# Thirty-two experts in 12 units instead of 13: four more of them in blocks of 64 rows

## The chip, the cores and the metric

The kernel runs on one core of one Trainium2 chip. Its time is device microseconds of one execution, from launch to end; lower is better. Five engines take part: TensorE (PE, with its weight loads as PEld), VectorE (DVE), ScalarE (ACT), GpSimd (POOL), and SyncE (SP), which issues the DMAs. Each works through its own list of instructions in order.

## The reference, cut to what matters

Two transformer blocks over 512 tokens of 1024 columns, in fp32. The change lies in the first block's mixture of experts:

```python
logits = xf @ w_router + b_router                 # 512 tokens, 32 experts
top_val, top_idx = lax.top_k(logits, 4)           # four experts a token: 2048 pairs
gates = softmax(top_val)
# for each expert, over its tokens:
hu = xb @ w_up[e] + b_up[e]                       # 1024 -> 2048 columns
act = x_glu * sigmoid(1.702 * x_glu) * (x_lin + 1)   # x_glu, x_lin: clipped halves of hu
y = act @ w_down[e] + b_down[e]                   # 1024 -> 1024
# a token's four rows, times their gates, are added up
```

How many tokens an expert gets depends on the data. With the inputs that the reference draws, its router gives the experts, after the first two (numbers 0 and 1, with 53 and 122 tokens), in falling order: 192, 133, 105, 104, 95, 87, 84, 79, 77, 73, 70, 67 (these are the ranks 2 to 13), 64, 63, 60, 53 (ranks 14 to 17), then 53, 50, 49, 48 down to 10 (ranks 18 to 31).

## The kernel before, in words

Matmuls are made of fp32r products: each operand is split in a high part and a low part, and a product is hi·hi + hi·lo + lo·hi (`mm3`, L290 to L292). The weights of an expert, 12 MB, come in 12 tiles of 128x2048 by DMA into a ring of six. ACT copies each tile into its high part `wh` (L281), and DVE subtracts that to give the low part `wl` (L286). Of an expert's 12 tiles, two are subtracted on POOL instead (L284).

Experts are worked in the order of a list, `units`. A unit is 256 rows of gathered tokens (`xT`, one buffer), cut in blocks. A block has 128 or 64 rows, all of one expert. There are three kinds of unit: a **pair** is two experts with 128 rows each; a **mixed** unit is one with 128 rows and two with 64; a **dual** unit is one expert with 128 + 64 rows and one with 64. `cap` says how many tokens of each rank have a place in these blocks. Tokens beyond it go to further blocks of 128 rows, which a loop on the chip works through after the second unit, as often as a number counted from the data says (`NXi`); each pass loads that expert's weights again through two half tiles.

For each unit, DVE makes one-hot columns (`hot`, L1083), PE gathers the tokens with them (L1125), and ACT and DVE copy the halves into `xT` (L1130). The small instructions L1100 to L1111 make each block's row numbers and gates. All of this for the next unit is issued during the current one. Then per expert: `expert_up` in four chunks of 256 hidden columns, `split_T`, and `expert_down` while the next expert's `expert_up` runs.

A block of 128 rows and one of 64 differ in these lines:

- PE: with 128 rows each step is the three matmuls L290 to L292. With 64 rows the hi and lo columns of the rows lie side by side, so that one matmul makes hi·hi and lo·hi in the two halves of the partitions, and a second one hi·lo: two matmuls (L1173, L1174, or L1168 and L1171 in the first step).
- DVE, per chunk, with 128 rows: L1208, L1210 and L1212 read the sum where it lies, in PSUM (`bank_hu`), and L1211 reads SBUF. With 64 rows the two halves are added first: ACT copies one into SBUF (`ft`, L1204), DVE adds the other (L1205), and L1208, L1210 and L1212 read `ft`.
- Behind: `split_T` has one DVE instruction L1230 for 64 rows and two for 128. A block of 64 is gated with two ACT and two DVE instructions (L1248, L1249), one of 128 with two ACT instructions (L1259).

The order of the instructions on each engine is fixed when the program is built, by a scheduler with its own estimate of durations; across the engines they wait for each other by semaphores.

Of the kernel before, what the change touches and what calls it, by code (L numbers as in the profile page):

```python
# [16 lines left out]
T = 512  # L17
# [5 lines left out]
SMALL = 18  # the experts by rank: from 2 up to 192 tokens for two of them, 64 from this one on, else 128  # L23
# [204 lines left out]
def tile_block(ctx, tc, A, out, dbg=None):  # L228
# [23 lines left out]
    # eight banks of PSUM, in groups that are used in turn  # L252
# [83 lines left out]
    def gemv(src, cofs, gp, bufs):  # L336
        """silu(c) @ src; columns 256 q .. 256 q + 255 end up in row 32 q"""
# [9 lines left out]
    def gemv_split(src, cofs, gp, ring_raw, nv=4):  # L347
        """the same, with the products and most of the sums on the other engines"""
# [35 lines left out]
    def mod_row(i, src, cofs, gp, bias, plus=0.0, mul=None, how="split"):  # L384
        """row i of md_d: (silu(c) @ src + bias + plus) * mul"""
# [82 lines left out]
    # gains and biases of the second block's norms, times sqrt(2) for the residual  # L468
# [33 lines left out]
    # gates of the delta rule  # L502
# [54 lines left out]
    def front(p):  # L557
        """doubled silu of the convolutions, inverse norms, the triangular systems"""
# [181 lines left out]
    # sliding-window attention; the logits of a head are kept in units of its slope  # L740
# [89 lines left out]
    # row slot * T + token of y_d; the last two experts' first tokens, of the slots 2 and 3, do not pass through it  # L830
# [11 lines left out]
    # output projection: the columns of the window's attention first  # L842
# [29 lines left out]
    # gated norm of the delta rule's output  # L872
# [29 lines left out]
    # residual, second norm, router  # L902
# [14 lines left out]
    # the norm's gain goes into the router's weights; the shift's share of the logits  # L917
# [18 lines left out]
    # those that are read last come first, away from the room of the experts' weights  # L936
# [7 lines left out]
    M = Z[:, :, 0:32]  # a token's chosen experts; then its gates, then its places  # L944
# [21 lines left out]
    # the experts' input bias in two parts, the columns' second half 64 rows further on  # L966
# [9 lines left out]
    def half_out(tb, ps, half):  # L976
        """half the columns of the residual, their share of its square and, before the norm's factor, of the logits"""
# [56 lines left out]
    # routing  # L1034
# [17 lines left out]
    # one plus a pair's place among its expert's tokens, 0 for the pairs that are not chosen  # L1052
# [10 lines left out]
    # units of 256 rows; a block of rows is an expert's rank, its columns in the unit, and the places that it leaves out  # L1063
# [6 lines left out]
    def mixed(a, b):  # L1070
        return [(a, 0, 128, 0), (b, 128, 64, 0), (b + 1, 192, 64, 0)]

    units = [pair_of(0), mixed(4, 20), mixed(5, 22), dual(2, 18), pair_of(6), mixed(8, 24), pair_of(9),
             mixed(11, 26), dual(3, 19), pair_of(12), mixed(14, 28), pair_of(15), mixed(17, 30)]
# [5 lines left out]
    def hot_cols(pos, hot):  # L1080
        """a block's rows of h2 as one-hot columns"""
        for tb in range(NTB):
            vec.tensor_scalar(out=hot[tb], in0=iob[:, 0:hot[tb].shape[1]], scalar1=pos[:, tb:tb + 1], scalar2=None,  # L1083
                              op0=OP.is_equal)
        return hot
# [9 lines left out]
    def slots(hot, Rsel):  # L1095
        """a block's rows of y_d and its gates; the gates of 64 rows twice"""
# [20 lines left out]
    def gather_T(hot, X, runs):  # L1117
        """hi and lo of the transposed rows of h2 that the one-hot columns select"""
# [14 lines left out]
    def rows_in(X, blk):  # L1133
        """the stationary operands of a block in X: hi, lo, and both side by side"""
        o, n = 2 * blk[1], blk[2]
        return n, lambda k: X[:, k, o:o + n], lambda k: X[:, k, o + n:o + 2 * n], lambda k: X[:, k, o:o + 2 * n]
# [22 lines left out]
    pools = [(4,), (2,)]  # the parts of an expert's weights that Pool helps to split  # L1159

    def prod(o, rows, k, w, first, last, then=None):
        """one step of the sum over k; with 64 rows, lo * hi comes out 64 rows below"""
# [16 lines left out]
    def expert_up(wsrc, bsel, rows, get=fetch):  # L1179
        """an expert's activations, in chunks of 256 of its hidden columns"""  # L1180
# [34 lines left out]
    def split_T(src, to=None):  # L1215
        """the stationary operands of the transposed activations"""
# [28 lines left out]
    def gated(yb, y, gc, s):  # L1245
        """gate times 64 rows in two parts"""
# [4 lines left out]
    def expert_out(y, sl, r, yb=None):  # L1251
        """gates a block's rows; the function that it returns writes them to y_d"""
# [14 lines left out]
    def add_rows(y, gc, hot, tiles):  # L1267
        """the factors of the product that adds the gated rows of a block of 64 to their tokens: its one-hot rows, and
        hi and lo; a row's two parts are two terms of the sum"""
# [19 lines left out]
    def block_rows(blk):  # L1289
        """a block's one-hot columns, its rows of y_d and its gates"""  # L1290
# [7 lines left out]
    def ranked(rank):  # L1298
        """the weights and the bias of the expert of a rank"""
# [23 lines left out]
    # the experts' ranks: 0 and 1 for the first two, the others by their tokens; M, gates and places in their order  # L1323
# [44 lines left out]
    # a pair's slot is its expert's place by rank among the token's four, counted from 1  # L1368
    vec.tensor_tensor_scan(out=jv, data0=seg, data1=M2.rearrange("p t e -> p (t e)"), initial=0.0,
                           op0=OP.mult, op1=OP.add)  # L1370
    # slot records per (token, expert): the pair's row / 16, its remainder, gate, 1
# [9 lines left out]
    def lists():  # L1381
        """the blocks beyond the experts' own: ranks, experts, offsets of their places, and the number of them"""
# [9 lines left out]
        # a block per partition: its rank is the number of ranks whose blocks all come before it  # L1392
# [4 lines left out]
        # places less 128 times the blocks before in the expert, less what its own hold  # L1397
# [23 lines left out]
    # experts  # L1421
# [3 lines left out]
    def begin(src, ready, ahead):  # L1425
        """the first weights of a block from what was loaded before"""
# [673 lines left out]
```

## Time and profile before

| | |
|---|---|
| median of 3 runs | 3288.72 us (3272.14 to 3291.38) |
| span of the profiled execution | 3273.7 us |
| stretch of the experts (460 to 1893 us) | 1433.2 us |
| PE, DVE, ACT, POOL busy in that stretch | 1264.0, 1349.2, 885.1, 601.6 us |
| DMA in that stretch | 287 GB/s, share 0.77 |

The page gives no time of the profiled execution apart from its span. The stretch of the experts begins when the first one-hot columns are made, and ends with the last `ma` of the last expert. A busy time is the time in which an engine had an instruction under way; an instruction that is held up by something else counts as busy too. The four engines overlap, so the times don't add up to the stretch.

### The profile page before, as it was taken

What the parts mean: (1) busy time and instruction counts of PE and PEld (TensorE: products, weight loads), DVE (VectorE), ACT (ScalarE), POOL (GpSimd) and SP (SyncE); (2) the same over time, 40 slices, a digit from 0 to 9 for tenths busy, and PEclk for the clock granted to TensorE, in tenths of its full rate; (3) what the DMA queues carried; (4) which work ended last, traced back from release to release, by engine and by line L of the source; (5) the groups of instructions that cost most, each with busy time, mean ns of one, the idle gap of its engine ahead of it and who ended that gap; (6) DMA issues with size and microseconds to landing.
All of it is one profiled execution on the core that took longest, in us unless ns stands there. A gap on an engine that the chain in (4) does not pass through costs nothing.

```text
span 3273.7 us, 37859 instructions
## 1 busy us (share of the span) xinstructions
PE 2902.4 (89%) x13632; PEld 2225.4 (68%) x13632; DVE 2627.4 (80%) x3392; ACT 1597.7 (49%) x1960; POOL 1181.6 (36%) x531
## 2 busy tenths in 40 slices
PE   6889988888899898999989759889999889889997
PEld 4667866655677566667667537577777767678886
DVE  5986479989999999999998985686756888875456
ACT  4433344666666656666666544442223645533231
POOL 2330165334443343344434562233323243442223
PEclk9999979989999999999999879989999999989999
DMA  7552346778688778778878754345532322223321
GB/s 264 182 176 87 106 169 236 296 274 314 248 305 304 287 290 303 280 271 302 305 284 311 276 195 161 116 147 199 178 128 89 112 63 92 83 84 100 100 92 56
DMA packets 127201, 643.73 MB, mean 197 GB/s; under 512 B 17142, under 2 KB 18122, under 8 KB 77856
## 3 DMA queue, kind: packets, MB, share of 16 engines
q1 hardware_dynamic: 122064, 632.27, 53.8%
q0 software_dynamic: 4800, 8.46, 0.7%
q8 instruction: 109, 1.79, 0.2%
q14 instruction: 84, 0.69, 0.1%
q10 hardware_dynamic: 144, 0.52, 0.0%
HBM read 624.42 MB, written 21.59 MB: 197 GB/s over the span
## 4 chain that ended last, share of the span: by engine, by line
PE 38%; DVE 26%; issue 7%; ACT 4%; DMA 2%; POOL 1%; DVEq 0%; ACTq 0%; SPq 0%; POOLq 0%
DVE wl L286 9%; PE bank_d L290 4%; PE bank_d L292 4%; PE bank_d L291 4%; PE bank_u L290 3%; PE bank_u L292 3%; PE bank_u L291 3%; DVE ma L1211 3%; ACT wh L281 2%; PE bank_hu L290 2%; PE bank_hu L291 2%; PE bank_hu L292 1%; DVE ma L1208 1%; PE bank_tr L1125 1%; PE bank_hu L1173 1%
## 5 line engine op out<-in xcount | busy, mean ns | idle before, releaser
L281 ACT CAST wh<-raw 128x2048 fp32r<-128x2048 f32 (+1 forms) x615 | 958.0, 1579 | 528.5 <-PE bank_u L291 177.7
L286 DVE TENSOR_TENSOR wl<-raw,wh 128x2048 fp32r<-128x2048 f32 (+2 forms) x521 | 1065.1, 2052 | 149.0 <-ACT wh L281 147.0
L284 POOL TENSOR_TENSOR wl<-raw,wh 128x2048 fp32r<-128x2048 f32 (+1 forms) x94 | 443.0, 4715 | 659.8 <-ACT wh L281 603.1
L1682 POOL TENSOR_TENSOR h2h<-h2h,yt 128x512 f32<-128x512 f32 x161 | 237.5, 1482 | 679.5 <-DVE yt L1681 669.5
L1681 DVE TENSOR_TENSOR yt<-bank_d,G 128x512 f32<-128x512 f32 x168 | 113.2, 686 | 182.9 <-PE bank_d L292 180.1
L291 PE MATMUL bank_u<-h_lo,wh 128*128 128x512 f32 (+1 forms) x680 | 251.3, 370 | 9.8 <-DVE h_lo L1666 9.8
L290 PE MATMUL bank_u<-h_hi,wh 128*128 128x512 f32 (+1 forms) x680 | 252.2, 373 | 6.3 <-ACT wh L281 3.2
L292 PE MATMUL bank_u<-h_hi,wl 128*128 128x512 f32 (+1 forms) x680 | 251.6, 371 | 0.0
L291 PE MATMUL bank_hu<-wl,xT 128*128 128x512 f32 x576 | 236.2, 411 | 14.9 <-DVE wl L286 9.6
L290 PE MATMUL bank_hu<-wh,xT 128*128 128x512 f32 x576 | 233.5, 410 | 0.0
L292 PE MATMUL bank_hu<-wh,xT 128*128 128x512 f32 x576 | 231.4, 403 | 0.0
L1262 POOL TENSOR_TENSOR yb<-yb,g2bc 128x1024 f32<-128x1024 f32 (+1 forms) x32 | 108.9, 3404 | 282.3 <-ACT yb L1259 201.8
L1173 PE MATMUL bank_hu<-wl,xT 128*64 128x512 f32 x448 | 191.2, 427 | 21.0 <-DVE wl L286 20.6
L290 PE MATMUL bank_d<-wh,a 128*128 128x512 f32 x512 | 202.5, 396 | 5.6 <-DVE yt L1681 3.5
L291 PE MATMUL bank_d<-wl,a 128*128 128x512 f32 x512 | 200.9, 393 | 0.0
L292 PE MATMUL bank_d<-wh,b 128*128 128x512 f32 x512 | 197.5, 392 | 0.0
L1174 PE MATMUL bank_hu<-wh,xT 128*128 128x512 f32 x448 | 188.5, 421 | 0.0
L1209 ACT ACTIVATE mb<-ma 128x256 f32<-128x256 f32 (+1 forms) x136 | 56.6, 417 | 265.4 <-DVE ma L1208 245.0
L1211 DVE SCALAR_TENSOR_TENSOR ma<-mb,ma 128x256 f32<-128x256 f32 (+1 forms) x136 | 153.6, 1129 | 8.4 <-ACT mb L1209 8.2
L291 PEld LDWEIGHTS bank_u<-h_lo,wh 128*128 128x128 f32 x680 | 130.8, 192 | 32.5 <-DVE h_lo L1666 10.5
L290 PEld LDWEIGHTS bank_u<-h_hi,wh 128*128 128x128 f32 x680 | 130.6, 193 | 28.4 <-ACT wh L281 3.6
L292 PEld LDWEIGHTS bank_u<-h_hi,wl 128*128 128x128 f32 x680 | 130.7, 192 | 22.3
(626 smaller groups left out, 6572.5 us busy)
## 6 DMA issues: line engine op xcount, KB each, us to landing
raw<-in_w_up_dram SPq DMA_DIRECT2D x256, 1024.0 KB, 4.9
raw<-in_w_down_dram SPq DMA_DIRECT2D x128, 1024.0 KB, 5.1
raw<-in_mlp_w_dram SPq DMA_DIRECT2D x128, 512.0 KB, 4.4
graw<-in_ada_w_dram SPq DMA_DIRECT2D x72, 512.0 KB, 4.1
graw<-in_w_ada_dram SPq DMA_DIRECT2D x48, 512.0 KB, 4.6
raw<-in_ada_w_dram SPq DMA_DIRECT2D x24, 512.0 KB, 4.2
raw<-in_rnn_w_in_dram SPq DMA_DIRECT2D x24, 512.0 KB, 3.8
raw<-in_w_in_dram SPq DMA_DIRECT2D x22, 512.0 KB, 4.2
```

Of the source, the lines that this page charges most:

```text
L281: act.copy(out=h, in_=r)
L284: pool.tensor_tensor(out=l, in0=r, in1=h.bitcast(F), op=OP.subtract)
L286: vec.tensor_tensor(out=l, in0=r, in1=h.bitcast(F), op=OP.subtract)
L290: pe.matmul(out=o, lhsT=lhs[0], rhs=rhs[0], start=first, stop=False)
L291: pe.matmul(out=o, lhsT=lhs[0], rhs=rhs[1], start=False, stop=False)
L292: pe.matmul(out=o, lhsT=lhs[1], rhs=rhs[0], start=False, stop=last)
L1173: pe.matmul(out=o[0:64], lhsT=hi(k), rhs=w[1], start=False, stop=False)
L1174: pe.matmul(out=o, lhsT=both(k), rhs=w[0], start=False, stop=last)
L1211: vec.scalar_tensor_tensor(out=a, in0=b, scalar=1.0, in1=a, op0=OP.add, op1=OP.mult)
L1262: pool.tensor_tensor(out=yb[0:r], in0=yb[0:r], in1=g2bc[0:r], op=OP.mult)
L1681: vec.tensor_tensor(out=t, in0=ps, in1=G[:, cs], op=OP.mult)
L1682: eng.tensor_tensor(out=xs[tb][:, cs], in0=xs[tb][:, cs], in1=t, op=OP.add)
```

## The change

The constant SMALL goes from 18 to 14, so that ranks 14 to 17 have a cap of 64 tokens instead of 128, and the list of units is written anew. The last unit's first expert, before which the experts' output bias is issued, is now found from the list. The other hunks of the diff drop comments.

```diff
-SMALL = 18  # the experts by rank: from 2 up to 192 tokens for two of them, 64 from this one on, else 128
+SMALL = 14
...
-    units = [pair_of(0), mixed(4, 20), mixed(5, 22), dual(2, 18), pair_of(6), mixed(8, 24), pair_of(9),
-             mixed(11, 26), dual(3, 19), pair_of(12), mixed(14, 28), pair_of(15), mixed(17, 30)]
+    units = [pair_of(0), mixed(4, 16), mixed(5, 18), dual(2, 14), mixed(6, 20), mixed(7, 22), mixed(8, 24), dual(3, 15),
+             mixed(9, 26), mixed(10, 28), pair_of(11), mixed(13, 30)]
...
-            if rank == 17:
+            if rank == units[-1][0][0]:
                 expert_bias()
```

In kinds: before P M M D P M P M D P M P M, now P M M D M M M D M M P M (P pair, M mixed, D dual). Blocks of 128 rows go from 18 to 14, blocks of 64 from 16 to 20. The number of blocks stays 34, and so does that of the experts.

Two places show how the instructions move. The first four units have the kinds that they had, so the first difference in kind is the fifth unit.

DVE in the last chunks of the fifth unit's last expert, while the sixth unit's tokens are copied into `xT`; before (rank 7, 128 rows; names: `ma` the activations, `mb` a work tile, `bank_hu` the sum in PSUM, `ft` its folded copy in SBUF):

```order
L1210 TENSOR_SCALAR bank_hu<-bank_hu 128x256
L1211 SCALAR_TENSOR_TENSOR ma<-mb,ma 128x256
L1208 TENSOR_SCALAR ma<-bank_hu 128x256
L1212 SCALAR_TENSOR_TENSOR ma<-bank_hu,ma 128x256
L1210 TENSOR_SCALAR bank_hu<-bank_hu 128x256
L1130 CAST xT<-bank_tr 128x2x128
L1130 CAST xT<-bank_tr 128x2x2x64
L286 TENSOR_TENSOR wl<-raw,wh 128x2048
L1211 SCALAR_TENSOR_TENSOR ma<-mb,ma 128x256
L1212 SCALAR_TENSOR_TENSOR ma<-bank_hu,ma 128x256
```

and in the changed kernel at the same place (rank 21, 64 rows):

```order
L1211 SCALAR_TENSOR_TENSOR ma<-mb,ma 64x256
L1130 CAST xT<-bank_tr 128x2x128
L1130 CAST xT<-bank_tr 128x2x2x64
L286 TENSOR_TENSOR wl<-raw,wh 128x2048
L1212 SCALAR_TENSOR_TENSOR ma<-ft,ma 64x256
L1205 TENSOR_TENSOR ft<-bank_hu,ft 64x512
L1130 CAST xT<-bank_tr 128x2x128
L1130 CAST xT<-bank_tr 128x2x2x64
L1208 TENSOR_SCALAR ma<-ft 64x256
L1210 TENSOR_SCALAR ft<-ft 64x256
```

The copies into `xT` and the subtraction L286 stand where they stood, between the chunks. A chunk has five DVE instructions instead of four, and L1208, L1210 and L1212 read `ft` instead of `bank_hu`.

PE in the first chunks of the fifth unit's second expert; before (rank 7, 128 rows):

```order
L290 MATMUL bank_hu<-wh,xT 128x512
L1100 MATMUL bank_tr<-R,hot 64x4 x3
L1227 MATMUL bank_tr<-ident,ma 128x128 x2
L1100 MATMUL bank_tr<-R,hot 64x4 x5
L290 MATMUL bank_hu<-wh,xT 128x512
L291 MATMUL bank_hu<-wl,xT 128x512
L292 MATMUL bank_hu<-wh,xT 128x512
```

and in the changed kernel (rank 20, 64 rows):

```order
L1173 MATMUL bank_hu<-wl,xT 64x512
L1174 MATMUL bank_hu<-wh,xT 128x512
L1100 MATMUL bank_tr<-R,hot 64x4 x8
L1168 MATMUL bank_hu<-wh,xT 128x512
L1187 MATMUL bank_hu<-bup,selE 64x512
L1173 MATMUL bank_hu<-wl,xT 64x512
L1174 MATMUL bank_hu<-wh,xT 128x512
```

A step of the sum has two matmuls instead of three, and the bias L1187 comes after the first of them instead of ahead of the chunk.

## Rows read from the trace of the kernel before

**Rows 1.** The page's first line, the profiled execution's span.

```profile
span 3273.7 us, 37859 instructions
```

**Rows 2.** Busy time in the experts' stretch: length, then engines, clock, DMA.

```profile
460.00:1893.20 1433.20, 1264.00 (x5762) 927.62 (x5762) 1349.21 (x1479) 885.07 (x783) 601.56 (x142) 0.95 0.77 287
```

**Rows 3.** The same for single units (pair, mixed, pair, mixed) and one expert.

```profile
core 0: us, PE busy (x) PEld busy (x) DVE busy (x) ACT busy (x) POOL busy (x), PEclk, DMA share, GB/s
926.20:1008.00 81.80, 77.26 (x373) 58.49 (x373) 79.58 (x91) 53.15 (x43) 34.66 (x10) 1.00 0.75 285
1008.00:1137.20 129.20, 114.64 (x517) 83.19 (x516) 123.49 (x122) 84.57 (x78) 50.02 (x12) 0.96 0.83 306
1137.20:1223.40 86.20, 78.54 (x358) 59.17 (x358) 83.70 (x92) 51.84 (x43) 35.42 (x8) 0.95 0.78 285
1223.40:1354.30 130.90, 113.45 (x527) 82.03 (x526) 124.67 (x133) 84.31 (x79) 43.02 (x12) 0.96 0.80 296
1008.00:1053.90 45.90, 44.76 (x207) 34.93 (x205) 42.74 (x45) 29.24 (x29) 14.39 (x4) 1.00 0.85 313
```

**Rows 4.** DVE lines of a block, by tile, 460 to 1905: min/median/max ns.

```profile
L1205 DVE TENSOR_TENSOR ft<-bank_hu,ft x64: 669/672/683, 625.2 to 1888.2; 64x512 f32<-64x512 f32 x64
L1208 DVE TENSOR_SCALAR ma<-bank_hu x72: 402/410/425, 500.5 to 1789.8; 128x256 f32<-128x256 f32 x72
L1208 DVE TENSOR_SCALAR ma<-ft x64: 271/276/4610, 628.7 to 1889.2; 64x256 f32<-64x256 f32 x64
L1210 DVE TENSOR_SCALAR bank_hu<-bank_hu x72: 410/418/433, 501.3 to 1790.3; 128x256 f32<-128x256 f32 x72
L1210 DVE TENSOR_SCALAR ft<-ft x64: 273/276/2429, 628.9 to 1889.4; 64x256 f32<-64x256 f32 x64
L1211 DVE SCALAR_TENSOR_TENSOR ma<-mb,ma x136: 402/409/5491, 508.9 to 1892.8; 128x256 f32<-128x256 f32 x72, 64x256 f32<-64x256 f32 x64
L1212 DVE SCALAR_TENSOR_TENSOR ma<-bank_hu,ma x72: 402/416/427, 509.7 to 1793.1; 128x256 f32<-128x256 f32 x72
L1212 DVE SCALAR_TENSOR_TENSOR ma<-ft,ma x64: 401/407/4803, 641.8 to 1893.3; 64x256 f32<-64x256 f32 x64
L1230 DVE TENSOR_TENSOR aT<-bank_tr,aT x52: 668/676/692, 531.6 to 1898.0; 128x512 fp32r<-128x512 f32 x52
L1249 DVE SCALAR_TENSOR_TENSOR yb<-bank_y,gc,ft x24: 729/732/734, 696.2 to 1719.7; 64x512 f32<-64x512 f32 x24
```

**Rows 5.** DVE groups by form, 460 to 1910: busy us, mean ns | idle before.

```profile
L1211 DVE SCALAR_TENSOR_TENSOR ma<-mb,ma 128x256 f32<-128x256 f32 x72 | 89.0, 1236 | 0.9 <-ACT mb L1209 0.7
L1211 DVE SCALAR_TENSOR_TENSOR ma<-mb,ma 64x256 f32<-64x256 f32 x64 | 64.6, 1009 | 7.5 <-ACT mb L1209 7.5
L1208 DVE TENSOR_SCALAR ma<-ft 64x256 f32<-64x256 f32 x64 | 63.3, 990 | 0.3
L1212 DVE SCALAR_TENSOR_TENSOR ma<-ft,ma 64x256 f32<-64x256 f32 x64 | 57.8, 904 | 0.5
L1130 DVE CAST xT<-bank_tr 128x256 fp32r<-128x256 f32 x64 | 23.8, 411 | 3.1 <-PE bank_tr L1125 2.6 <-PE bank_hu L1174 0.5
L1130 DVE CAST xT<-bank_tr 128x512 fp32r<-128x512 f32 x20 | 13.6, 680 | 10.0 <-PE bank_tr L1125 8.1 <-PE bank_hu L1174 1.9
```

**Rows 6.** Timeline, POOL and DVE at 866 us: start, us, engine, line.

```profile
866.69 4.61 POOL L284 TENSOR_TENSOR wl<-raw,wh 128x2048 fp32r<-128x2048 f32 x1 [23.09 <-ACT wh L281]
866.96 4.62 DVE L1211 SCALAR_TENSOR_TENSOR ma<-mb,ma 64x256 f32<-64x256 f32 x1 [2.53 <-ACT mb L1209]
```

**Rows 7.** One line's view, POOL's subtraction, 460 to 1905: min/median/max ns.

```profile
L284 POOL TENSOR_TENSOR wl<-raw,wh x72: 4517/4692/12082, 461.7 to 1897.8; 128x2048 fp32r<-128x2048 f32 x72
```

**Rows 8.** Timeline, PE: first and eleventh matmul of a dense run in a pair.

```profile
987.44 0.40 PE L292 MATMUL bank_hu<-wh,xT 128*128 128x512 f32 x1
...
989.77 0.40 PE L290 MATMUL bank_hu<-wh,xT 128*128 128x512 f32 x1
```

**Rows 9.** Splitting the weights on ACT and DVE, by form, 460 to 1910.

```profile
L281 ACT CAST wh<-raw 128x2048 fp32r<-128x2048 f32 x384 | 721.3, 1901 | 128.2 <-PE bank_hu L292 51.6 <-issue 38.7 <-PE bank_hu L1174 19.3
L286 DVE TENSOR_TENSOR wl<-raw,wh 128x2048 fp32r<-128x2048 f32 x310 | 762.2, 2466 | 39.2 <-ACT wh L281 38.9
```

## The prediction

> **What bounds the kernel now.** I read the windows first. The change touches only the experts' stretch, 1433.2 of 3273.7 us [rows 1, 2]. There DVE is busy for 1349.2 us, 94%, PE for 1264.0, 88%, ACT for 885.1 and POOL for 601.6, and the DMA share is 0.77 [rows 2]. The single units say the same more sharply: a pair takes 81.8 or 86.2 us with DVE busy for 79.6 or 83.7 of them, so DVE idles 2.2 to 2.5 us; a mixed unit takes 129.2 or 130.9 us with DVE busy for 123.5 or 124.7, so it idles 5.7 to 6.2 us [rows 3]. (A unit here runs from the last L1211 of one unit to that of the next. Further on in the stretch, a pair at 1458.6 us and a mixed unit at 1540.5 us repeat the first two windows to 0.1 us, and a pair at 1669.7 us the third.) Only in one place does PE lead: in the first expert of a mixed unit, with 128 rows, it is busy for 44.8 of 45.9 us, DVE for 42.7 [rows 3]. So DVE bounds the stretch, and PE takes some 5 us at the head of each mixed unit.
>
> Then the durations of DVE's lines, since a busy engine may be a held one. L1208 on `ft` has a median of 276 ns and a maximum of 4610; L1208 on `bank_hu` never leaves 402 to 425 [rows 4]. The timeline shows why: an L1211 that begins 0.27 us after a POOL subtraction lasts 4.62 us instead of its median 0.41, and ends 0.28 us after POOL does [rows 4, 6]. So medians price DVE's own work, and the means [rows 5] hold the waits for POOL besides.
>
> **The change part by part.** Three pairs go, two mixed units come; first, second, last and both dual units keep their kinds. Experts, weight tiles, their splits on ACT, DVE and POOL, SP's loads, and the blocks' 34 sets of row numbers and gates stay as many. I make the sum in two ways.
>
> *By instructions.* Four blocks go from 128 rows to 64. A chunk of 128 rows costs DVE 410 + 418 + 409 + 416 = 1653 ns, one of 64 rows 672 + 276 + 276 + 409 + 407 = 2040 ns [rows 4]; with four chunks, two L1230 against one (676 ns) and two L1249 (732 ns) against none, a block of 128 comes to 6.61 + 1.35 = 7.96 us, one of 64 to 8.16 + 0.68 + 1.46 = 10.30. Four times 2.34 is +9.4 us. Copies into `xT`: a pair has four of 680 ns, a mixed unit eight of 411 [rows 5]; −12 × 0.68 + 16 × 0.411 = −1.6 us. One-hot columns for 64 rows are narrower than for 128; I cost that at nothing. DVE's own work: +7.8 us. DVE's idle time, by unit: 2 × 5.9 − 3 × 2.35 = +4.7 us, which holds what PE, ACT and the single buffer `xT` make DVE wait for at a unit's head. Sum: **+12.5 us**.
>
> *By units.* Mean pair 84.0, mean mixed unit 129.8 (129.2 twice and 130.9) [rows 3]: 2 × 129.8 − 3 × 84.0 = +7.6. But a window also holds the preparation of the next unit's blocks. A mixed unit takes 130.9 us ahead of a dual unit (three blocks to prepare), 129.2 ahead of a pair (two): 1.7 us a block. All pairs here prepare three. Booked to the unit that owns the blocks, a pair costs 84.0 − 1.7 = 82.3, a mixed unit 129.2 + 1.7 = 130.9: 2 × 130.9 − 3 × 82.3 = **+14.9 us**.
>
> *PE.* 576 matmuls L290 to L292 go, and 384 of L1168 to L1174 come, 192 fewer; the pitch in a dense run is 2.33 us for ten, 0.233 each [rows 8], so 44.7 us. One gather less is 64 matmuls of half the columns, by estimate 7.5 us. Together −52 us. I cost it at nothing on the end, because DVE is the later engine in all but the first expert of a mixed unit, and of that kind there will be eight instead of six. If that cover is gone (DVE waiting for PE more than the windows show), it is the first rival.
>
> *ACT* gets 16 more copies L1204; at DVE's price for the same 64x512, 0.672 us [rows 4], that is 11 us, in a stretch where ACT idles for 548 [rows 2]. Nothing; without cover, up to 11 us, since each DVE fold L1205 waits for one. POOL's 34 products with the gate and its subtractions stay as many.
>
> I take **+13 us**, between the two ways. On the profiled execution that is 3273.7 + 13 = 3287; that execution lies 15 us below the median of 3288.7, on which I forecast 3302.
>
> **The rivals.**
>
> *PE gives the time back.* Were the stretch paced by PE, the 52 us would come off: 3237 us, −1.6%. For it: ACT's splits wait 70.9 us in all for matmuls to free `wh` [rows 9], so PE's lateness does reach the others. Against: DVE has at most 1433 − 1349 = 84 us of idle time in the whole stretch, the start-up in it, and its own work grows. 13%.
>
> *POOL holds DVE more often.* A 64-row chunk has more instructions that can be held: by mean less median, L1211 of a 128-row block loses 4 × 0.83 = 3.3 us; a 64-row block loses 4 × (0.60 + 0.71 + 0.50) = 7.2 us at L1211, L1208 and L1212 [rows 4, 5]. If these holds add up, four blocks cost 4 × 3.9 = 15.6 us more: 3317 us, +0.9%. [...] Against it: POOL's work, 72 subtractions of 4.7 us [rows 7] among it, stays as it is, and a hold that misses one instruction falls on the next. If the holds added up by block, an expert of a mixed unit would keep DVE busy 2/3 × (2.34 + 3.9) = 4.2 us longer than one of a pair; it does so by 41.2 to 41.6 against 40.8, under 1 us [rows 3]. 13%.
>
> *A further block is run.* The caps of ranks 14 to 17 drop to 64, and the reference gives rank 14 exactly 64 tokens. One token more there, by a router logit that comes out otherwise on the chip, and the loop makes a pass. The 384 weight copies of the trace are 32 × 12, so it makes none now [rows 9]. Its pass has one buffer for each of a tile's parts, so split and matmuls follow one another: 12 × (1.90 + 2.47 [rows 9] + 24 × 0.233 [rows 8]) = 120 us; hidden like an expert of a pair it would be 41 [rows 3]. I take 120, since nothing runs beside the loop: 3422 us, slower by 4%. It decides at the 65th token. Against it: the count is at the cap, not over it, and a pass needs a changed choice between a token's fourth and fifth expert. 5%.
>
> **How the numbers follow.** The forecast has 65%. Its own range goes from 3282 to 3320: the units' own spread gives 2 × 129.2 − 3 × 86.2 = 0 to 2 × 132.6 − 3 × 81.8 = +20 us (132.6: 130.9 and one block's preparation), ACT's 11 us may come on top, and the fast end gets 7 us for PE relief at the heads of units. The last 4% are for an order of the instructions that I have not foreseen, on either side. The range of 8 in 10 takes in the holds (3317) and a part of PE's relief: 3258 to 3326. Out of it stay PE's full 52 us and the further block. The three runs differ by 0.6%, so about 1% can be told from no change: 33 us. Faster by over 1% (below 3256): PE's rival with most of its chance, and 1% for the order: 13%. Slower by over 1% (above 3322): the block's 5%, the upper tail of the holds 4%, and 2% from the forecast and the order: 11%. Within 1%: 76%.
>
> **What would show it.** In the changed profile a mixed unit should again take 129 to 133 us, with DVE busy for 95% of it, and DVE in the stretch should be busy for about 8 us longer in spite of one unit less; PE's busy time should fall by some 50 us and its idle time grow by more. L281 should still count 384. I am wrong if mixed units that follow one another take under 125 us with PE's busy share unchanged (PE had paced them), if the mean of L1208 and L1212 on `ft` rises above 1.0 us while no other line's falls (holds add up), or if L281 counts more.

## The result, and the profile after

The changed kernel takes 3307.6 us (median of 4 runs, 3306.5 to 3310.2), the kernel before beside it 3285.5 (4 runs, 3272.1 to 3291.4): a ratio of 1.0078, 95% interval 1.0058 to 1.0098. That is 22 us slower, within 1%, and 6 us above the forecast of 3302. The page's first line of the changed kernel:

```profile
span 3306.0 us, 37430 instructions
```

The experts' stretch ends at the last L1211 and the rest follows; columns as in [rows 2], changed kernel:

```profile
460.00:1917.50 1457.50, 1245.95 (x5542) 894.31 (x5542) 1361.17 (x1513) 889.49 (x801) 613.55 (x142) 0.92 0.75 282
1917.50:3306.00 1388.50, 1251.69 (x5549) 998.28 (x5548) 946.78 (x1276) 531.75 (x819) 456.29 (x295) 0.94 0.35 114
```

Against [rows 2] the stretch is 24.3 us longer (the rest of the span by 8.0 more: the profiled execution of before is at the fast end of its runs). Read three columns. DVE is busy for 1361.2 us instead of 1349.2, so +12.0. Its idle time goes from 84.0 to 96.3, so +12.3. And PE's busy time falls by 18 us only, though 192 matmuls and a gather are gone, with a granted clock of 0.92 instead of 0.95.

Single units, changed kernel, same columns, from the first dual to the last pair (D M M M D M M P):

```profile
core 0: us, PE busy (x) PEld busy (x) DVE busy (x) ACT busy (x) POOL busy (x), PEclk, DMA share, GB/s
825.10:927.60 102.50, 95.34 (x445) 68.16 (x445) 97.11 (x121) 61.12 (x60) 44.92 (x8) 0.96 0.73 273
927.60:1058.10 130.50, 112.61 (x501) 78.67 (x501) 121.03 (x133) 83.27 (x76) 59.22 (x14) 0.93 0.75 280
1058.10:1193.00 134.90, 111.05 (x489) 79.16 (x489) 127.43 (x135) 84.35 (x78) 46.38 (x12) 0.89 0.76 290
1193.00:1321.30 128.30, 106.50 (x466) 74.65 (x464) 125.41 (x130) 82.11 (x74) 51.07 (x12) 0.92 0.80 293
1321.30:1431.50 110.20, 98.44 (x449) 70.17 (x449) 102.56 (x125) 61.51 (x59) 40.84 (x8) 0.94 0.71 261
1431.50:1562.70 131.20, 114.95 (x516) 80.19 (x515) 119.80 (x133) 85.81 (x78) 60.13 (x14) 0.93 0.75 275
1562.70:1690.30 127.60, 106.03 (x446) 74.77 (x444) 124.79 (x119) 80.21 (x69) 49.68 (x12) 0.91 0.80 298
1690.30:1779.20 88.90, 79.94 (x364) 60.78 (x363) 85.81 (x94) 52.99 (x44) 31.76 (x8) 0.94 0.76 286
```

Five mixed units take 127.6 to 134.9 us, 130.5 in the mean, against 129.2 to 130.9 in [rows 3]: 3.5 us more for the five. The second dual takes 110.2 us and the pair 88.9 (a pair's mean was 84.0): 5.9 and 4.9 us more, in units that kept their kind. The second dual before:

```profile
1354.30:1458.60 104.30, 96.89 (x448) 70.25 (x448) 101.31 (x115) 62.54 (x59) 45.15 (x8) 0.97 0.76 276
```

No mixed unit reaches 0.96 of the clock, as [rows 3] show it. The two behind a dual idle DVE for 9.5 and 11.4 us instead of 5.7 to 6.2; the other three for 2.8 to 7.5. Before the change a pair stood behind each dual, so these two units have a new neighbour.

DVE's lines, changed kernel, columns as in [rows 5], 460 to 1930 us:

```profile
L286 DVE TENSOR_TENSOR wl<-raw,wh 128x2048 fp32r<-128x2048 f32 x310 | 773.5, 2503 | 55.8 <-ACT wh L281 55.0 <-issue 0.4
L1211 DVE SCALAR_TENSOR_TENSOR ma<-mb,ma 64x256 f32<-64x256 f32 x80 | 82.6, 1032 | 7.6 <-ACT mb L1209 7.2 <-issue 0.3
L1212 DVE SCALAR_TENSOR_TENSOR ma<-ft,ma 64x256 f32<-64x256 f32 x80 | 75.7, 946 | 0.8
L1211 DVE SCALAR_TENSOR_TENSOR ma<-mb,ma 128x256 f32<-128x256 f32 x56 | 66.4, 1186 | 0.3 <-ACT mb L1209 0.3
L1208 DVE TENSOR_SCALAR ma<-ft 64x256 f32<-64x256 f32 x80 | 61.7, 771 | 0.6
```

The mean of L1208 on `ft` has fallen from 990 ns to 771, those of L1211 on 64 rows, L1212 and L286 rose by 23 to 42, and that of L1211 on 128 rows fell from 1236 to 1186: the holds lie elsewhere, and are hardly more. Summed over all DVE records of the stretch, duration less the median of the same line, tiles and shape comes to some 316 us before and 319 after.

L281 over the whole run still counts 384, so no further block was run:

```profile
L281 ACT CAST wh<-raw 128x2048 fp32r<-128x2048 f32 x384 | 721.8, 1901 | 126.6 <-PE bank_hu L292 46.4 <-PE bank_hu L1174 29.6 <-issue 27.4
```

The view of waits says what ended DVE's idle time (line waited for: us, times, longest). Its first row in the stretch, kernel before:

```profile
DVE wl L286 <- ACT wh L281: 38.9, 32, 4.6
```

and the changed kernel:

```profile
DVE wl L286 <- ACT wh L281: 55.0, 34, 4.0
```

These 16 us are more than DVE's whole growth of idle time. They lie in few places. Past 600 us the longest such wait before is 1.8 us; the changed kernel has five of 2.8 to 4.0 us, 17.0 us in sum, at 936.95, 1022.45, 1155.57, 1441.38 and 1525.66. Timeline of the changed kernel ahead of the third: POOL, then DVE, PE and ACT (start, us, engine, line; in brackets the idle time ahead and its releaser):

```profile
1135.74 5.59 POOL L284 TENSOR_TENSOR wl<-raw,wh 128x2048 fp32r<-128x2048 f32 x1 [12.99 <-ACT wh L281]
...
1136.82 4.66 DVE L1208 TENSOR_SCALAR ma<-ft 64x256 f32<-64x256 f32 x1
...
1143.17 0.42 DVE L1212 SCALAR_TENSOR_TENSOR ma<-ft,ma 64x256 f32<-64x256 f32 x1
...
1155.57 2.82 DVE L286 TENSOR_TENSOR wl<-raw,wh 128x2048 fp32r<-128x2048 f32 x1 [2.87 <-ACT wh L281]
...
1143.64 0.34 PE L1227 MATMUL bank_tr<-ident,ma 64*128 64x64 f32 x2 [3.62 <-DVE ma L1212]
...
1144.94 0.79 PE L291 MATMUL bank_y<-wl,aT 128*128 128x512 f32 x1
...
1145.96 0.63 PE L291 MATMUL bank_y<-wl,aT 128*128 128x512 f32 x1
1146.39 0.63 PE L292 MATMUL bank_y<-wh,aT 128*128 128x512 f32 x1
...
1150.98 0.40 PE L291 MATMUL bank_y<-wl,aT 128*128 128x512 f32 x1
1151.22 0.40 PE L292 MATMUL bank_y<-wh,aT 128*128 128x512 f32 x1
1151.45 0.39 PE L290 MATMUL bank_y<-wh,aT 128*128 128x512 f32 x1
...
1152.36 1.39 ACT L1259 ACTIVATE yb<-bank_y,gc 128x512 f32<-128x512 f32 x2 [2.77 <-PE bank_y L292]
1153.64 3.70 ACT L281 CAST wh<-raw 128x2048 fp32r<-128x2048 f32 x2
```

and its windows over the same stretch:

```profile
1134.00:1139.60 5.60, 5.46 (x23) 4.37 (x24) 5.60 (x4) 1.66 (x1) 3.86 (x1) 1.00 1.00 415
1139.60:1144.00 4.40, 0.76 (x4) 0.20 (x2) 4.30 (x8) 1.25 (x3) 1.73 (x1) 1.00 0.87 320
1144.00:1151.00 7.00, 6.46 (x17) 5.05 (x18) 6.04 (x6) 5.56 (x4) 0.00 (x0) 0.51 0.57 213
1151.00:1156.00 5.00, 5.00 (x26) 3.66 (x25) 2.13 (x2) 3.63 (x4) 2.18 (x1) 1.00 0.99 406
```

A POOL subtraction holds DVE's L1208 for 4.66 us. L1212 behind it is late, and PE stands 3.62 us for it ahead of the transposes L1227. Then the granted clock is at half for 6.8 us (0.51 in the window): matmuls follow one another every 0.43 us, and every 0.23 from 1151.22 on, where it is at 1.00 again. From 1144.94 to 1150.98 fourteen steps take 6.0 us; at 0.233 [rows 8] they would take 3.3, by estimate. So the sum in `bank_y` is late by 2.8 us, ACT's L1259 waits 2.77 us for it, and the split that stands behind L1259 in ACT's list comes when DVE has waited 2.87 us. Ahead of the waits at 1022.45 (4.01 us) and 1525.66 (2.81 us) PE stood 4.41 and 4.42 us for a subtraction on POOL, and half the clock followed too, for 6.8 and 3.4 us.

The other two, 3.65 us each, stand at the heads of the two mixed units behind a dual. There ACT gates the dual's rows ahead of its split, and PE is busy without a gap at the full clock:

```profile
920.00:937.00 17.00, 17.00 (x96) 13.70 (x95) 11.55 (x23) 10.82 (x15) 2.94 (x2) 1.00 0.64 236
1425.00:1441.40 16.40, 16.40 (x94) 13.24 (x93) 10.42 (x21) 10.79 (x15) 2.92 (x2) 1.00 0.59 216
```

So 9.7 us of the 17 stand behind a hold by POOL and the half clock together, and 7.3 behind the new neighbours.

By the records of the granted clock, the stretch stood at half for 149 us in all before and 242 after. I call half of that the clock's loss: 75 and 121 us (0.95 and 0.92 of the two windows).

### The profile page after: what moved, and what is told of

Its sections match the earlier page's. It is cut to its first block, busy times and chain, and to the rows that moved or that the text cites. A ratio compares the mean times of both kernels' runs of the same rounds, so it can differ in the third digit from the quotient of the medians.

```text
span 3306.0 us, 37430 instructions
## 1 busy us (share of the span) xinstructions
PE 2896.4 (88%) x13408; PEld 2201.2 (67%) x13408; DVE 2638.9 (80%) x3416; ACT 1600.7 (48%) x1976; POOL 1195.7 (36%) x531
## 4 chain that ended last, share of the span: by engine, by line
PE 34%; DVE 27%; issue 8%; ACT 4%; DMA 4%; POOL 2%; DVEq 0%; SPq 0%; ACTq 0%; POOLq 0%
DVE wl L286 10%; PE bank_d L290 4%; PE bank_d L292 4%; PE bank_d L291 4%; PE bank_u L292 3%; PE bank_u L290 3%; PE bank_u L291 3%; DVE ma L1211 3%; DMA graw<-in_ada_w_dram 2%; ACT wh L281 2%; POOL wl L284 1%; DVE ma L1212 1%; PE bank_hu L291 1%; PE bank_hu L290 1%; PE bank_hu L292 1%
## 5 line engine op out<-in xcount | busy, mean ns | idle before, releaser
L281 ACT CAST wh<-raw 128x2048 fp32r<-128x2048 f32 (+1 forms) x615 | 958.7, 1579 | 550.4 <-PE bank_u L291 194.9
L286 DVE TENSOR_TENSOR wl<-raw,wh 128x2048 fp32r<-128x2048 f32 (+2 forms) x521 | 1076.4, 2074 | 173.3 <-ACT wh L281 171.6
L284 POOL TENSOR_TENSOR wl<-raw,wh 128x2048 fp32r<-128x2048 f32 (+1 forms) x94 | 452.3, 4814 | 663.8 <-ACT wh L281 570.9
L1173 PE MATMUL bank_hu<-wl,xT 128*64 128x512 f32 x560 | 239.5, 428 | 26.8 <-DVE wl L286 26.7
L1174 PE MATMUL bank_hu<-wh,xT 128*128 128x512 f32 x560 | 236.2, 422 | 0.0
L1262 POOL TENSOR_TENSOR yb<-yb,g2bc 64x1024 f32<-64x1024 f32 (+1 forms) x32 | 122.2, 3818 | 282.5 <-ACT yb L1259 149.0
L291 PE MATMUL bank_hu<-wl,xT 128*128 128x512 f32 x448 | 187.2, 419 | 25.4 <-DVE wl L286 22.5
L290 PE MATMUL bank_hu<-wh,xT 128*128 128x512 f32 x448 | 185.0, 417 | 0.0
L292 PE MATMUL bank_hu<-wh,xT 128*128 128x512 f32 x448 | 183.9, 412 | 0.0
L1209 ACT ACTIVATE mb<-ma 64x256 f32<-64x256 f32 (+1 forms) x136 | 56.6, 416 | 238.6 <-DVE ma L1208 200.7
L1211 DVE SCALAR_TENSOR_TENSOR ma<-mb,ma 64x256 f32<-64x256 f32 (+1 forms) x136 | 149.0, 1096 | 8.0 <-ACT mb L1209 7.5
L1174 PEld LDWEIGHTS bank_hu<-wh,xT 128*128 128x128 f32 x560 | 115.2, 206 | 56.6 <-issue 13.3
```

Source lines behind the costliest of these rows:

```text
L281: act.copy(out=h, in_=r)
L284: pool.tensor_tensor(out=l, in0=r, in1=h.bitcast(F), op=OP.subtract)
L286: vec.tensor_tensor(out=l, in0=r, in1=h.bitcast(F), op=OP.subtract)
L290: pe.matmul(out=o, lhsT=lhs[0], rhs=rhs[0], start=first, stop=False)
L291: pe.matmul(out=o, lhsT=lhs[0], rhs=rhs[1], start=False, stop=False)
L292: pe.matmul(out=o, lhsT=lhs[1], rhs=rhs[0], start=False, stop=last)
```

## The experiments

The theory: the blocks cost DVE some 10 us of its own, and the rest of the 22 us comes from the clock. With less to do, PE stands more often for DVE and POOL, is granted half the clock more often, and is then late itself at the heads of units. Rivals: holds by POOL; the order of the units; DVE's own work alone; the order of the instructions. A padding matmul below is a third matmul in a step of two; it adds the product hi·lo of that step once more to the sum. The scheduler moves instructions in each variant, which no run held constant: of the changed kernel's 1511 DVE and 801 ACT instructions in the stretch, the longest sequence that e8 has in the same order holds 1256 and 717. Lines are 5 further down in kernels with padding.

| kernel | median us | ratio to before (95%) | stretch us | PE, DVE busy us | clock | loss us |
|---|---|---|---|---|---|---|
| before | | | 1433.2 | 1264.0, 1349.2 | 0.95 | 75 |
| changed | 3307.6 | 1.0078 (1.0058 to 1.0098) | 1457.5 | 1246.0, 1361.2 | 0.92 | 121 |
| e3_pe_pad | 3290.2 | 1.0020 (1.0007 to 1.0033) | 1441.8 | 1265.6, 1355.8 | 0.93 | 96 |
| e4_nofold | 3270.2 | 0.9951 (0.9934 to 0.9969) | 1411.8 | 1222.0, 1309.3 | 0.93 | 96 |
| e1_nopool_after | 3230.2 | 0.9827 (0.9803 to 0.9852) | 1392.0 | 1224.1, 1271.8 | 0.93 | 99 |
| e2_nopool_before | 3220.7 | 0.9802 (0.9780 to 0.9825) | 1386.4 | 1252.5, 1256.4 | 0.95 | 68 |
| e5_rows_only | 3292.3 | 1.0045 (1.0029 to 1.0061) | 1440.3 | 1237.2, 1355.5 | 0.93 | 100 |
| e6_order | 3304.0 | 1.0066 (1.0047 to 1.0085) | 1459.8 | 1242.6, 1355.0 | 0.92 | 115 |
| e7_pad_small | 3331.7 | 1.0163 (1.0146 to 1.0180) | 1477.8 | 1268.8, 1350.5 | 0.91 | 128 |
| e8_warm | 3282.3 | 1.0004 (0.9992 to 1.0017) | 1432.8 | 1282.4, 1350.1 | 0.95 | 67 |
| e9_nopool_warm_after | 3220.7 | 0.9820 (0.9803 to 0.9836) | 1383.3 | 1273.4, 1273.4 | 0.96 | 58 |
| e10_nopool_warm_before | 3217.0 | 0.9803 (0.9787 to 0.9819) | 1387.0 | 1298.4, 1264.8 | 0.96 | 55 |
| e11_warm_before | 3285.6 | 1.0009 (0.9996 to 1.0023) | 1436.5 | 1307.6, 1343.9 | 0.96 | 63 |
| e12_warm_more | 3290.4 | 1.0026 (1.0015 to 1.0037) | 1437.3 | 1359.0, 1347.4 | 0.96 | 51 |

The first four, then e5 to e8, then e9 to e12 shared their runs of the kernel before: 3284.6, 3281.6 and 3282.3 us. The changed kernel was not run again beside them, so its distance to a variant is best read from the two ratios. The stretch and what follows in the table come from the profiled execution, which lies 8 us above the median in e5, 10 us above it in e11 and near the fast end in the kernel before; what lies behind the stretch differs by 17 us between the kernels that leave POOL as it was (1380.5 to 1397.6). The losses named in the expectations are 6 to 15 us larger than those of the table, since they take in the whole of a record that begins ahead of the stretch.

**e3: PE's work put back.** The changed kernel with a padding matmul in each step of the four experts that went from 128 rows to 64: 192 more.

```diff
             pe.matmul(out=o[0:64], lhsT=hi(k), rhs=w[1], start=False, stop=False)
+            if pad[0]:
+                pe.matmul(out=o[0:64], lhsT=hi(k), rhs=w[1], start=False, stop=False)
...
+            pad[0] = 14 <= rank < 18
```

> The changed kernel with PE's saving put back: in the experts of ranks 14 to 17 each step issues the hi*lo matmul of 64 rows a second time, so that a step has three matmuls as with 128 rows (192 more, 44.7 us at the dense pitch of 0.233; the small term is counted twice). DVE, ACT, POOL and the DMAs do what they did. If DVE paces the stretch, the time stays that of the changed kernel within 10 us, 3298 to 3318. If PE paces it (the rival in which PE gives time back, only less of it than something else took), 30 to 45 us come on top: 3338 to 3352. If the lower granted clock of the changed kernel (0.92 in the stretch against 0.95) comes from PE's idle time, the clock should rise to 0.94 or more and the time may even fall by up to 10 us.

44.7 us of PE's work were added, and the kernel became 17 us faster, 3290.2; the expectation allowed for 10. The added work is no cost on this layout. The loss fell from 121 to 96 us and DVE's idle time from 96.3 to 86.0; the clock of 0.93 is short of the 0.94 that was expected.

**e4: DVE's fold left out.** The changed kernel without L1205 in 64-row blocks; the product lo·hi of the experts' first layer is left out of them.

```diff
-                    vec.tensor_tensor(out=ft, in0=hu[0:64], in1=ft, op=OP.add)
-                    hu = ft
+                hu = hu[0:64]
```

> The changed kernel with DVE's fold L1205 left out in all 20 blocks of 64 rows: L1208, L1210 and L1212 read the first half of the sum where it lies in PSUM, as with 128 rows (the lo*hi term of expert_up is left out). ACT's copy L1204 stays. DVE's own work: 80 folds of 0.672 us go, L1208 and L1210 cost 0.134 and 0.142 us more each, L1212 0.009: 80 x (0.672 - 0.285) = -31 us. If DVE paces the stretch and holds by POOL only move to other instructions, the time falls by 25 to 35 us, to 3273 to 3283, and the holds' sum stays near 318 us. If holds add up by exposed instruction, L1208 and L1212 lose 39 + 43 us of them too: -80 to -110 us, 3198 to 3228. If PE or the heads of the units pace it, no change: 3300 to 3312.

3270.2, 37 us less than the changed kernel, just below the range given for a stretch that DVE paces. The 80 folds are 54 us by their duration of 672 ns [rows 4], but L1208 and L1210 take longer on `bank_hu` (with 128 rows 410 and 418 ns, against 276 on `ft` [rows 4]), so that DVE's own work falls by 29 us. DVE is busy for 52 us less and the stretch 46 us shorter: DVE bounds it, and most of what DVE is spared comes back, with PE's matmuls as many. Holds fell from 319 to 288 us, so some of them go with L1208 and L1212, which no longer read `ft`; the far larger gain that the rival on holds asked for did not come.

**e1 and e2: POOL's subtractions on DVE.** From the second unit on, 60 of the stretch's 71 subtractions go from POOL to DVE, in the changed kernel (e1) and in the kernel before (e2).

```diff
-        pools[:] = [(1, 3, 5, 7), (0, 2)] if u == 0 else [(4,), (2,)]
+        pools[:] = [(1, 3, 5, 7), (0, 2)] if u == 0 else [(), ()]
         if not nxt:
-            pools[1] = (0,)
+            pools[1] = ()
```

> The changed kernel with POOL's weight subtractions from the second unit on (60 of 72) done by DVE. [...] If DVE is truly held while POOL works, as long rows beside POOL's show, two thirds of the 318 us of holds go, 214 us, so that DVE's busy time falls by some 75 us and the time by 30 to 75 us, to 3233 to 3278, until PE paces the stretch. If the long rows were waits that something else sets, the time grows by up to 137 us, to 3445.

> The kernel before with the same move. With DVE relieved by some 75 us, PE, which is busy for 1264 of 1433 us here, should pace more of the stretch than in the changed layout, which has 52 us less for it. So, if the layout loses because DVE paces, it should lose less or gain once DVE does not: the changed layout with this move minus this kernel is then -30 to +8 us instead of +22. If the layout's cost has nothing to do with which engine paces (a cost at the heads of units, say), the difference stays +15 to +25 us.

The expectation's two thirds are 60 subtractions of 4.69 us [rows 7], 281 of the some 418 us that POOL's subtractions and products with the gate take in the kernel before, by their medians; its 137 us are 60 subtractions on DVE at 2.28. Both are far faster: 77 us off the changed kernel, where 30 to 75 were expected, and 64 off the one before. DVE takes on 60 subtractions of 2.28 us and is still busy for 89 and 93 us less, since the holds drop to some 87 and 81. DVE's groups in e1, columns as in [rows 5]:

```profile
L286 DVE TENSOR_TENSOR wl<-raw,wh 128x2048 fp32r<-128x2048 f32 x373 | 883.5, 2377 | 70.3 <-ACT wh L281 70.3
L1212 DVE SCALAR_TENSOR_TENSOR ma<-ft,ma 64x256 f32<-64x256 f32 x80 | 41.2, 515 | 0.4
L1211 DVE SCALAR_TENSOR_TENSOR ma<-mb,ma 64x256 f32<-64x256 f32 x80 | 36.2, 452 | 0.4 <-ACT mb L1209 0.4
...
L1208 DVE TENSOR_SCALAR ma<-ft 64x256 f32<-64x256 f32 x80 | 28.1, 352 | 0.5
```

The means of the three are down to 352 to 515 ns from 771 to 1032. Between the layouts 9.5 us are left instead of 22, in ratios whose intervals overlap. That lies between the two cases of e2's expectation (at most +8, or +15 to +25) and decides neither. The drop from 319 to 87 us shows that the 60 subtractions on POOL made most of the holds; by what means the two engines hold one another is not shown.

**e5: the blocks alone.** The 13 units of before, with ranks 14 to 17 in 64-row blocks.

```diff
-             mixed(11, 26), dual(3, 19), pair_of(12), mixed(14, 28), pair_of(15), mixed(17, 30)]
+             mixed(11, 26), dual(3, 19), pair_of(12), small(14, 28, 29), small(15, 16), small(17, 30, 31)]
...
+        gather_T([hots[-1][:, tb, 0:w] for tb in range(NTB)], X, runs)
```

> The kernel before, in its 13 units, with ranks 14 to 17 in blocks of 64 rows: the units (14, 28, 29), (15, 16) and (17, 30, 31) get 192, 128 and 192 rows. So the blocks are those of the change, without its new layout. DVE's own work grows by 4 x 2.34 = 9 us as in the change; PE saves 45 us of the 52. If the blocks make the cost (DVE's own work and what PE's clock takes), the time lies near the changed kernel: 3297 to 3310. If the new layout makes it (mixed units one behind the other, and behind dual units), 3285 to 3296.

3292.3, 11 us over its runs of before: half of the 22, and by the expectation (3285 to 3296) a sign that the new layout makes the rest. DVE's own work (each line's count by its median) rose by some 9 us, against 9.4 forecast for four blocks. The clock is at 0.93 here already, with four blocks' matmuls gone and 26 us more of loss. But DVE's idle time is 84.8 us, as before the change (84.0): this loss did not reach DVE. The growth of 12.3 us came only with the 12 units.

**e6: another order of the units.** The changed kernel with the pair behind the first dual.

```diff
-    units = [..., dual(2, 14), mixed(6, 20), mixed(7, 22), mixed(8, 24), dual(3, 15), mixed(9, 26), mixed(10, 28), pair_of(11), ...]
+    units = [..., dual(2, 14), pair_of(6), mixed(8, 20), mixed(9, 22), dual(3, 15), mixed(10, 24), mixed(11, 26), mixed(12, 28), ...]
```

> The changed kernel with its 12 units in another order: the pair stands behind the first dual unit (ranks 6 and 7), four mixed units in a row end the list. The work on every engine is the same. If the cost is in the work (DVE's own, PE's idle time and clock), the time stays within 8 us of the changed kernel's 3308. If it is in the order of the units and of the instructions in them, it can move by 10 to 20 us either way.

3304.0: 4 us less than the changed kernel, in intervals that overlap, and as far above its runs of before (22 us). This other order of the units costs the same.

**e7: small padding.** e3 with its matmuls cut to 64 columns: as many instructions, an eighth of the columns.

```diff
+                pe.matmul(out=o[0:64, 0:64], lhsT=hi(k), rhs=w[1][:, 0:64], start=False, stop=False)
```

> The kernel with PE's saving put back (192 more matmuls in ranks 14 to 17, 3290 us) with each of these matmuls cut from 512 to 64 columns: as many instructions in the same steps, an eighth of PE's added work. If PE's added work itself made that kernel faster than the changed one, by keeping the granted clock up, most of the gain goes: 3300 to 3308, with 120 us or more lost to the half clock in the stretch (133 in the changed kernel, 102 with the full pads). If a lucky order of the instructions made it, which comes with their number, the time stays at 3286 to 3297.

e3's gain is gone, which speaks for the length of the matmuls and against their number. But e7 is also 24 us slower than the changed kernel, outside both ranges of the expectation. Its first row of DVE's waits:

```profile
DVE wl L286 <- ACT wh L281: 81.9, 46, 12.9
```

is up 27 us from 55.0, and holds one of 12.9. There a subtraction on POOL lasts 17.74 us, among DVE's instructions, instead of 4.69 [rows 7], and PE stands 10.16 us for it. The order of the instructions differs from e3's too, and moves the time by as much as the effect in question; so e7 doesn't show that the length alone made e3's gain.

**e8: padding where PE had room.** The changed kernel with padding in the third expert of seven of its mixed units: 336 matmuls, 78 us.

```diff
+    pad, warm = [False], (17, 19, 21, 23, 25, 27, 29)
...
+            pad[0] = rank in warm
```

> The changed kernel with the third matmul in the third expert of seven mixed units, where PE has most idle time, instead of in ranks 14 to 17: 336 more matmuls, 78 us of PE's work at the dense pitch; nothing else on DVE, ACT, POOL. If PE's idle time costs clock, and the clock costs time at the heads of the next units, the time lost to the half clock falls below 110 us and the kernel takes 3283 to 3298. If only DVE paces the stretch, 3300 to 3312. If PE paces it, 3330 or more.

3282.3: level with the kernel before, and just below the expected 3283 to 3298. Its stretch, and its mixed units behind the duals with the second dual between them:

```profile
460.00:1892.80 1432.80, 1282.37 (x5878) 917.06 (x5878) 1350.07 (x1515) 891.60 (x801) 583.46 (x142) 0.95 0.77 287
932.20:1055.80 123.60, 113.59 (x519) 78.36 (x518) 119.78 (x131) 82.70 (x75) 58.02 (x14) 0.97 0.80 297
1313.90:1415.70 101.80, 99.16 (x486) 71.29 (x485) 96.97 (x124) 62.66 (x63) 38.25 (x8) 1.00 0.74 275
1415.70:1539.70 124.00, 112.30 (x519) 77.68 (x518) 120.13 (x131) 82.68 (x75) 55.47 (x14) 0.99 0.79 293
```

The three units take 123.6, 101.8 and 124.0 us where the changed kernel took 130.5, 110.2 and 131.2, with PE busy for 113.6, 99.2 and 112.3 us instead of 112.6, 98.4 and 115.0, padding and all, at 0.97 to 1.00 of the clock. In the whole stretch PE got 78 us more to do and is busy for 36 more; its busy time at half the clock fell from 198 to 112 us, which gives the rest. DVE's wait for `wh` is back:

```profile
DVE wl L286 <- ACT wh L281: 40.6, 38, 4.7
```

Of the 24.7 us that the stretch lost, 13.6 are DVE's idle time, 11.1 its busy time, by holds, which fell from 319 to 308. Not all of it can be the clock's: the two waits of 3.65 us behind the duals are 1.11 us each here, with the clock full in both kernels, and ACT's list has one split more ahead of L1259 there. PE's wait for the `wl` of POOL also fell, from 38.5 to 11.6 us.

**e9 and e10: both edits together.** e1 with e8's padding (e9); e2 with padding in the third expert of five mixed units of before, 240 matmuls (e10). Nothing else differs from the edits above.

```diff
+    pad, warm = [False], (21, 23, 25, 27, 29)
...
-        pools[:] = [(1, 3, 5, 7), (0, 2)] if u == 0 else [(4,), (2,)]
+        pools[:] = [(1, 3, 5, 7), (0, 2)] if u == 0 else [(), ()]
```

> Both gains on the changed layout: POOL's weight subtractions on DVE (3230 us alone, with 113 us lost to the half clock in the stretch) and the third matmul in the third expert of seven mixed units (25 us alone). If the clock costs time at the heads of units there too, half to all of the 25 us come off: 3205 to 3218. If PE paces that kernel, whose DVE is less busy, the 78 us of added matmuls show: 3240 or more.

> The same two on the layout before (POOL's subtractions on DVE alone: 3221 us, 79 us lost to the half clock); 240 more matmuls, 56 us, in the third expert of five mixed units. Less clock to win and more work on PE: 3215 to 3230.

e9 takes 3220.7, 9.5 us less than e1, and e10 3217.0, 3.6 less than e2, in ratios whose intervals overlap. e9 was expected at 3205 to 3218, with at least half of the 25 us that the padding brought in e8; it brought less. With the clock at 0.96 in both and the 60 subtractions off POOL, the layouts differ by 3.7 us, and their intervals overlap. Both beat both kernels by some 2%; e10's ratio, 0.9803, is e2's 0.9802, so e2 is the version to take, without padding.

**e11: padding in the kernel before.** The same 240 matmuls, POOL as it was.

```diff
+    pad, warm = [False], (21, 23, 25, 27, 29)
```

> The kernel before with the third matmul in the third expert of five mixed units (240 more, 56 us), POOL unchanged. Before the change 85 us are lost to the half clock, as against 133 behind it. If the changed layout loses because of the clock, the kernel before has little to win: 3272 to 3290, so that with the pads in both the layouts are equal within 10 us. If the pads help by something else than the clock, they should help here as much, 20 us or more: below 3265.

3285.6, ratio 1.0009, as expected: no gain. The loss falls by 12 us, but DVE's idle time grows from 84.0 to 92.6. Padding and the higher clock, 0.96 instead of 0.95, bring nothing here; with padding in both, the layouts are level (e8 1.0004, e11 1.0009).

**e12: padding everywhere.** The changed kernel with padding in ranks 14 to 29: 768 matmuls, 179 us.

```diff
+    pad, warm = [False], tuple(range(14, 30))
```

> The changed kernel with the third matmul in all experts of ranks 14 to 29 (768 more, 179 us of PE's work, more than the 52 us that the change saves). The clock has little more to win than in the kernel with seven such experts (77 us lost), and PE begins to pace: its busy time goes over 1340 of some 1440 us. 3285 to 3320; below 3275 would say that PE has more free time than the windows show.

3290.4, within the expected range and still 17 us less than the changed kernel, but 8 more than e8: the loss is down to 51 us, and PE's busy time, 1359.0, now exceeds DVE's 1347.4.

## Why the prediction was right in its sum and wrong in one term

*What bounds the stretch.* DVE, as forecast: e4 got its 37 us by sparing DVE its folds, and the holds that went with them.

*DVE's own work, +7.8.* Right in its size. DVE's busy time rose by 12.0 us, of which the holds are some 3 and its own work some 9; the blocks alone brought as much in e5.

*Holds.* Costed at nothing, and some 3 us by the sums. The rival fails on its own terms: L1208's mean fell while others' rose, as the argument that a hold missing one instruction falls on the next had it. e4 shows that this argument isn't the whole of it: there 31 us of holds did go with their instructions. The whole of the holds was large, some 232 us of the stretch by e1. What the prediction left out is that PE waits for POOL's subtractions: 25.5 us in the stretch before, 38.5 after.

*The further block* was not run.

*DVE's idle time, +4.7.* This is the term that was mis-sized: it measured +12.3. I priced the new mixed units at what the old ones idled, and took PE's relief as worth nothing, hidden behind DVE. No run shows it worth more than nothing. Of 52 us that PE was spared, its busy time shows 18; about 34 went back to a lower granted clock (PE's busy time at half the clock rose from 119 to 198 us, 39 us by the pitch). "PE gives the time back", at 13%, did not come: 52 us less on PE made nothing faster. Nor did PE's busy time fall by some 50 us, as the prediction asked; its idle time grew by 42. Of its other signs, DVE's busy share of 95% in mixed units came in the mean (91 to 98%), but three of the five lie outside the 129 to 133 us.

The chain of causes is read in three places, 9.7 us of DVE's waits, and e3, e8 and e12 agree with it. PE stands for an activation or a split that a subtraction on POOL makes late. PE's wait for L1212 ahead of the transposes L1227 of 64-row blocks is the largest; before:

```profile
L1227 PE MATMUL bank_tr<-ident,ma 64*128 64x64 f32 x128 | 18.3, 257 | 24.9 <-DVE ma L1212 24.7 <-DVE h2l L1461 0.2
```

and after:

```profile
L1227 PE MATMUL bank_tr<-ident,ma 64*128 64x64 f32 x160 | 22.8, 254 | 44.9 <-DVE ma L1212 43.6 <-DVE h2l L1461 1.2
```

Then the clock is at half, and the matmuls whose sum ACT has to gate ahead of its next split come every 0.43 us instead of every 0.23. What sets the granted clock is not shown; that sparing PE might lower it, and cost time, should have stood among the rivals. What is shown is that on the changed layout kernels with padding of full length had a clock of 0.93, 0.95 and 0.96 instead of 0.92 (e3, e8, e12) and got 14 to 21 us back, each against its own runs of before, and the one with short padding didn't (0.91, e7). That DVE's 12.3 us hang on the clock is not shown. Against it stand e5, where 26 us more of loss cost DVE no idle time, and 7.3 us of waits behind duals at the full clock; and the order of the instructions moved with every edit, in e8 for at least 255 of DVE's 1511. Clock, new neighbours and order are not told apart.

*The sum* for the stretch was +12.5 by instructions, and 24.3 was measured: 7.6 us short in DVE's idle time, 4.2 in its busy time. The medians differ by 22 us, of which 13 were forecast. That the time came within 6 us of 3302 is in part luck: 3302 stood on a median before of 3288.7, which came out as 3285.5.

## What to carry to other kernels

Work taken off an engine that isn't the bound need not be free of effect: look at TensorE's granted clock in the stretch first, and ask what the engine will do with the time. Here 52 us less of work on PE went with a clock of 0.92 instead of 0.95, 42 us more of idle time on PE and 12.3 on DVE. When the longest instructions of one engine far exceed their median, look for what they coincide with, sum duration less median over the stretch, and price moving the other engine's work away: here that was worth 64 to 77 us, three times what was disputed. A term taken over from units "of the same kind" is to be read again under new neighbours and another clock: DVE's 5.7 to 6.2 us of idle time in a mixed unit became 9.5 and 11.4 behind a dual.

## What the runs showed of the hardware, unexpected

336 redundant 128x512 matmuls, 78 us of them, went with a kernel 25 us faster (e8), and 192 of 64 columns, in other experts, with one 24 us slower (e7). The granted clock rose from 0.92 to 0.95 with the former and fell to 0.91 with the latter; the order of the instructions changed in both. A subtraction of 4.7 us on POOL cost DVE more than doing it there in 2.28: 60 of them moved to DVE took 89 to 93 us off DVE's busy time. The hold went both ways: beside DVE's instructions, single subtractions on POOL lasted 12.60 us in the changed kernel, where their median is 4.67, and 17.74 in e7, and PE stood 4.41 and 10.16 us for them.
